# Hybrid decoder trunk: the four block sums of each up-weight pair in the second gated network made by transfers that add

## The chip, the cores and the metric

One core of a Trainium2 chip runs the whole program. The metric is device time in microseconds (us) for one execution. The kernel before takes 1214.67 us, the median of three runs (1213.35 to 1220.85). Engines are called PE (matrix), DVE (vector), ACT (scalar), POOL (GpSimd) and SP (the engine that only issues transfers here).

## The reference, cut to what matters

Two layers of width 1024 over 512 tokens: a state-space mixer, a gated network, an attention mixer, a gated network, each normed and with a residual. The change touches the gated networks, `conv_ffn`:

```python
def conv_ffn(h, w_up, conv_w, conv_b, w_down):
    up = h @ w_up                      # 1024 -> 2 * 2816
    a, b = jnp.split(up, 2, axis=-1)
    ap = jnp.pad(a, ((0, 0), (CONV_W - 1, 0), (0, 0)))
    a_conv = conv_b
    for i in range(CONV_W):
        a_conv = a_conv + ap[:, i:i + S] * conv_w[i]
    return (jax.nn.silu(a_conv) * b) @ w_down
```

Everything is float32 in and out.

## The kernel before, in words

Every float32 product is made of rounded halves: an operand is split into a high part (`w_hi`, made by ACT, a copy that rounds) and a low part (`w_lo`, made by DVE as operand minus high part), and three matmuls are added up (high by high, high by low, low by high). `put_parts` makes the two halves (L275 to L278).

The 2816 hidden features are 22 units of 128. Unit f has two tiles of up weights, 128 outputs of the convolved branch and 128 of the other, each 128 partitions by 8 blocks of 128 (512 KB). Units named in `plain` are multiplied directly (`product`, matmuls at L294, 512 columns). The other units go through `quarters` (L510): the pair of weight tiles is seen as a 2 by 2 matrix of half tiles a11, a12 (first output tile) and a21, a22 (second), the input as a 2 by 2 matrix of halves of the contraction and halves of the tokens, and seven products of half size are made instead of eight (matmuls at L550, 12 of 256 columns to a product). The scheme needs four sums of weight blocks, s1 = a21 + a22, s2 = s1 - a11, s3 = a11 - a21, s4 = a12 - s2, and four sums of input blocks t1 to t4, which `forms_x` makes once for a network (L493 to L506). The products follow each other on PE as a11, s1, a12, s2, s4, a22, s3. Tile `c` holds s1 and s2, tile `d` holds s3 and s4, both in the ring of buffers named `sums`, which has two buffers and which `forms_x` uses too. DVE makes the four sums (L518), then `parts` makes the halves of a, of c, of d and of a22. `copy` (L555) takes products out of PSUM through ACT (`nm_h`), DVE adds them (`nm_t`), and `gated` (L590) does the convolution, the gate and the split into `ghi` and `glo`.

The first network has 15 units of this kind, the second has 18, units 4 to 21 (`plain=(0, 1, 2, 3)`). The hidden units are taken in groups (6, 5, 6, 5 in the second network), and from the second group on each unit is followed by one or two column tiles of the down product of the group before (18 or 15 matmuls of 512 columns each, L294). Units 4 and 5 belong to the first group: nothing stands between them and unit 6.

Five rings set how far ahead work can run: `raw` (3 buffers, weights as loaded, L180 to L187), `w_hi` and `w_lo` (5 each), `sums`, and the PSUM ring `mm` (4 banks), of which a unit takes two (p1 and p5) and a column tile of the down product one. All engines and queues run in a fixed order, which a scheduler of the tile framework wrote at build time. SP issues all loads of the second network. POOL issues loads of modulation weights in the first network (`ada_raw`, L233) and has nothing to do in the second.

Of the kernel before, what the change touches and what calls it, by code (L numbers as in the profile page):

```python
# [8 lines left out]
F32 = mybir.dt.float32  # L9
F32R = mybir.dt.float32r  # L10
I32 = mybir.dt.int32
AF = mybir.ActivationFunctionType
ALU = mybir.AluOpType
# [4 lines left out]
P = 128  # L18
D = 1024
KT = D // P  # L20
# [46 lines left out]
def part_of(pool, shape, name, tag, bufs, aside=0):  # L67

    _, n, w = shape
    t = pool.tile([P, ROOM if bufs == WB else n * w + P], F32R, name=name, tag=tag, bufs=bufs)  # L70
    return t[:, aside:aside + n * w].rearrange("p (n w) -> p n w", w=w)


class Trunk:
# [401 lines left out]
    def forms_x(self, pool, x):  # L476

        nc = self.nc
        H, N = KT // 2, S // 2
        t1, t2 = HALVES  # L480
        normed = self.last_lo.ins
        b = []
        for j, n in enumerate(("ghi1", "glo1")):
            t = pool.tile([P, H, S], F32, name=f"x{j}", tag=n)
            for c in HALVES:
                k = slice(j * H, (j + 1) * H)
                with self.tc.issue_after(normed):
                    nc.vector.tensor_tensor(t[:, :, c], x[0][:, k, c].bitcast(F32), x[1][:, k, c].bitcast(F32), ALU.add)
                yield
            b.append(t)  # L490
        self.tx = {}

        def form(n, u, v):  # L493
            t = pool.tile([P, H, N], F32, name="sums", bufs=2)
            nc.vector.tensor_tensor(t, u, v, ALU.subtract)
            hi, lo = (pool.tile([P, H, N], F32R, name=m, bufs=4) for m in ("w_hi", "w_lo"))
            self.put_parts(hi, lo, t)
            self.tx[n] = hi, lo
            return t

        f1 = form(1, b[0][:, :, t2], b[0][:, :, t1])
        yield
        f2 = form(2, b[1][:, :, t2], f1)
        yield
        form(4, f2, b[1][:, :, t1])
        yield  # L506
        form(3, b[1][:, :, t2], b[0][:, :, t2])
        yield

    def quarters(self, pool, l, f, x, finish):  # L510

        nc = self.nc
        H, N = KT // 2, S // 2
        t1, t2 = HALVES
        a, b = (self.raw([P, KT, P], self.io["w_up"][l][2 * f + j]) for j in range(2))
        a11, a12, a21, a22 = a[:, :H], a[:, H:], b[:, :H], b[:, H:]
        c, d = (pool.tile([P, 2, H, P], F32, name="sums", bufs=2) for _ in range(2))
        sub = lambda o, u, v, op=ALU.subtract: nc.vector.tensor_tensor(o, u, v, op)  # L518
        w = {}
        copied = self.copied  # L520

        def parts(src, names, *where):
            hi, lo = (
                pool.tile([P, H * P + P], F32R, name=n, tag="e" + n)[:, ASIDE:ASIDE + H * P].rearrange("p (n w) -> p n w", w=P)
                if where else part_of(self.wpool, [P, len(names) * H, P], n, n, WB, ASIDE)
                for n in ("w_hi", "w_lo")
            )
            with self.behind(*copied):
                self.put_parts(hi, lo, src)
            for j, n in enumerate(names):  # L530
                w[n] = hi[:, j * H:(j + 1) * H], lo[:, j * H:(j + 1) * H]

        parts(a, ("a11", "a12"))
        sub(c[:, 0], a21, a22, ALU.add)
        sub(c[:, 1], c[:, 0], a11)
        parts(c.rearrange("p n k m -> p (n k) m"), ("s1", "s2"))
        sub(d[:, 1], a11, a21)
        sub(d[:, 0], a12, c[:, 1])
        parts(d.rearrange("p n k m -> p (n k) m"), ("s4", "s3"))
        parts(a22, ("a22",), pool)  # L540
        quarter = lambda k, t: tuple(v[:, k * H:(k + 1) * H, t] for v in x)
        xs = {"b11": quarter(0, t1), "b21": quarter(1, t1), "b22": quarter(1, t2)}
        for n, v in self.tx.items():
            xs[f"t{n}"] = v

        def times(o, wn, xn, first=True):
            (whi, wlo), (xhi, xlo) = w[wn], xs[xn]
            for k in range(H):
                for n, (wt, xt) in enumerate(((whi, xhi), (whi, xlo), (wlo, xhi))):
                    self.last_mm = nc.tensor.matmul(  # L550
                        o, wt[:, k], xt[:, k], start=(first and k == 0 and n == 0), stop=(k == H - 1 and n == 2),
                        skip_group_check=True,
                    )

        def copy(o, last=False):  # L555
            t = self.tmp.tile([P, N], F32, name="nm_h", bufs=4)
            a = nc.scalar.activation(t, o, AF.Copy)  # L557
            if last:
                self.copied = [a.ins]
            return t  # L560

        p1, p5 = (self.mm.tile([P, S], F32, name="mmp")[:, :N] for _ in range(2))
        p2, p4 = (self.aux.tile([P, S], F32, name="aux")[:, :N] for _ in range(2))
        oa, ob = (self.tmp.tile([P, S], F32, name="nm_t") for _ in range(2))
        times(p1, "a11", "b11")
        c1 = copy(p1)
        times(p5, "s1", "t1")
        c5 = copy(p5)
        times(p2, "a12", "b21")
        sub(oa[:, t1], p2, c1, ALU.add)  # L570
        times(p1, "s2", "t2", False)
        c2 = copy(p1, True)
        times(p5, "s4", "b22", False)
        sub(oa[:, t2], p5, c2, ALU.add)
        finish(2 * f, oa, slice(0, S))
        times(p4, "a22", "t4")
        c4 = copy(p4)
        times(p1, "s3", "t3", False)
        sub(ob[:, t2], p1, c5, ALU.add)
        sub(ob[:, t1], p1, c4)  # L580
        finish(2 * f + 1, ob, slice(0, S))

    def ffn(self, i, l, x, nxt, ticks=0, plain=None):

        nc, tc = self.nc, self.tc
        with tc.tile_pool(name=f"ffn{l}", bufs=1, reuse_waits="tile") as pool:
            self.bgpool = pool
            conv = pool.tile([P, 4, FT], F32, name="conv_wb")
            nc.sync.dma_start(conv, self.io["conv"][l])
            fill(pool, 1696)  # L590
# [5 lines left out]
            def gated(m, ps, cols):  # L596
# [25 lines left out]
            up = lambda fs, **k: self.product(  # L622
                self.io["w_up"][l], range(2 * fs[0], 2 * fs[-1] + 2), KT, x, gated,
                ticks=0 if plain else ticks, **k
            )
            last = len(groups) - 1
# [53 lines left out]
class Ew:  # L680
# [29 lines left out]
    def sub(self, a, b, out=None):  # L710
        return self.tt(a, b, ALU.subtract, out)
# [934 lines left out]
```

## Time and profile before

| what | value |
|---|---|
| median of 3 runs | 1214.67 us |
| the profiled execution, its own time | 1217.02 us |
| its span in the trace | 1215.2 us |
| granted TensorE clock, mean | 0.995 |
| PE busy | 1180.3 us, 97% |
| DVE busy | 1007.6 us, 83% |
| ACT busy | 609.8 us, 50% |
| POOL busy | 83.9 us, 7% |
| read from HBM | 175.57 MB |

The second gated network runs from about 860 us to the end of the span. In the views, "L518 DVE ... sums<-raw" is a group of instructions by its line in the program, engine, and output and input tiles; a wait "PE mmp L550 <- ACT nm_h L557" says that matmuls of line 550 stood until an instruction of line 557 on ACT was done. DMA times run from issue to landing.

### The profile page before, as it was taken

To read this page: it belongs to the slowest core of one execution; us is meant where nothing else is said; L and a number is where in the kernel's file an instruction comes from. 1 tells how busy PE (TensorE), PEld (TensorE's weight loads), DVE (VectorE), ACT (ScalarE), POOL (GpSimd) and SP (SyncE) were. 2 spreads that over 40 slices of the span, in tenths; PEclk is the share of its full clock that TensorE was granted. 3 is DMA by queue.
4 is the path that set the end of the run, shared out by engine and by line. 5 is a ranking of instruction groups with operands and counts; after the bars stand their busy time and mean duration, and the time that the engine had idled before them with its cause. 6 is when DMAs were issued, how large, how long until landed. Compare 5 with 4: busy or idle time off the path is not lost.

```text
span 1215.2 us, 20334 instructions
## 1 busy us (share of the span) xinstructions
PE 1180.3 (97%) x7793; PEld 1015.4 (84%) x7793; DVE 1007.6 (83%) x1872; ACT 609.8 (50%) x1156; POOL 83.9 (7%) x145
## 2 busy tenths in 40 slices
PE   7999999999999999999999999999999999999997
PEld 2566688898989899889899777878989999999987
DVE  7999977789899988898687578875899887888965
ACT  3644555336445454455443565654466554555543
POOL 0000000100000000000000333430000000000000
PEclk9999999999999999999999999999999999999999
DMA  9778786622455544553445543432213332333331
GB/s 348 243 250 261 233 294 220 210 77 70 136 179 164 189 155 148 169 168 106 126 153 180 172 153 130 148 108 88 89 53 113 112 119 90 103 104 109 109 100 70
DMA packets 74512, 183.81 MB, mean 151 GB/s; under 512 B 23231, under 2 KB 25631, under 8 KB 73391
## 3 DMA queue, kind: packets, MB, share of 16 engines
q1 hardware_dynamic: 68367, 161.02, 40.5%
q0 software_dynamic: 5760, 20.97, 5.4%
q8 instruction: 61, 1.00, 0.3%
q10 hardware_dynamic: 288, 0.52, 0.1%
q14 instruction: 36, 0.29, 0.1%
HBM read 175.57 MB, written 6.92 MB: 150 GB/s over the span
## 4 chain that ended last, share of the span: by engine, by line
PE 56%; issue 26%; DVE 8%; DMA 5%; ACT 2%; POOL 2%; SPq 0%; POOLq 0%; DVEq 0%; ACTq 0%
PE mmp L294 24%; PE mmp L550 11%; PE aux L550 4%; PE mmp L1366 3%; PE mmp L1174 2%; DVE w_lo L278 2%; PE mmp L1203 2%; POOL ada_raw L233 1%; PE aux L1505 1%; DMA ada_raw<-in_ada_t 1%; PE aux L1065 1%; PE mmp L1114 1%; PE aux L1057 1%; PE aux L978 1%; DMA yt<-s_yd 1%
## 5 line engine op out<-in xcount | busy, mean ns | idle before, releaser
L278 DVE TENSOR_TENSOR w_lo<-raw,w_hi 128x1024 fp32r<-128x1024 f32 (+4 forms) x173 | 183.3, 1064 | 37.6 <-ACT w_hi L277 31.8
L277 ACT ACTIVATE w_hi<-raw 128x1024 fp32r<-128x1024 f32 (+4 forms) x173 | 154.8, 904 | 105.4 <-PE mmp L294 48.6
L294 PE MATMUL mmp<-ghi,w_hi 128*128 128x512 f32 (+1 forms) x392 | 145.5, 371 | 0.0
L294 PE MATMUL mmp<-ghi,w_lo 128*128 128x512 f32 (+1 forms) x392 | 144.7, 369 | 0.7 <-DVE w_lo L278 0.6
L294 PE MATMUL mmp<-glo,w_hi 128*128 128x512 f32 (+1 forms) x392 | 145.1, 370 | 0.0
L294 PE MATMUL mmp<-a_hi,w_hi 128*128 128x512 f32 (+1 forms) x376 | 138.4, 371 | 1.5 <-ACT a_hi L433 1.5
L294 PE MATMUL mmp<-a_hi,w_lo 128*128 128x512 f32 (+1 forms) x376 | 136.2, 363 | 0.2 <-DVE w_lo L278 0.2
L294 PE MATMUL mmp<-a_lo,w_hi 128*128 128x512 f32 (+1 forms) x376 | 135.7, 362 | 0.0
L550 PE MATMUL mmp<-w_hi 128*128 128x256 f32 x396 | 109.7, 277 | 2.7 <-ACT nm_h L557 2.3
L550 PE MATMUL mmp<-w_hi,w_lo 128*128 128x256 f32 x396 | 109.5, 277 | 0.7 <-DVE w_lo L278 0.7
L550 PE MATMUL mmp<-w_lo,w_hi 128*128 128x256 f32 x396 | 109.4, 276 | 0.0
L557 ACT ACTIVATE nm_h<-mmp 128x256 f32<-128x256 f32 x99 | 37.2, 381 | 107.3 <-PE mmp L550 107.3
L278 DVE TENSOR_TENSOR w_lo<-sums,w_hi 128x1024 fp32r<-128x1024 f32 x74 | 90.0, 1219 | 0.0
L277 ACT ACTIVATE w_hi<-sums 128x1024 fp32r<-128x1024 f32 x74 | 77.0, 1055 | 23.7 <-DVE sums L518 21.7
L294 PEld LDWEIGHTS mmp<-ghi,w_lo 128*128 128x128 f32 x392 | 74.7, 190 | 13.8 <-DVE w_lo L278 1.5
L294 PEld LDWEIGHTS mmp<-ghi,w_hi 128*128 128x128 f32 x392 | 74.7, 191 | 11.5 <-ACT w_hi L277 0.2
L294 PEld LDWEIGHTS mmp<-glo,w_hi 128*128 128x128 f32 x392 | 74.8, 191 | 11.1
L294 PEld LDWEIGHTS mmp<-a_hi,w_hi 128*128 128x128 f32 x376 | 70.2, 188 | 13.8 <-issue 2.6
L294 PEld LDWEIGHTS mmp<-a_hi,w_lo 128*128 128x128 f32 x376 | 70.6, 188 | 12.2 <-DVE w_lo L278 1.2
L294 PEld LDWEIGHTS mmp<-a_lo,w_hi 128*128 128x128 f32 x376 | 70.7, 188 | 9.7
L362 DVE SCALAR_TENSOR_TENSOR h<-mmp,par,h 128x512 f32<-128x512 f32 (+1 forms) x100 | 68.0, 681 | 12.1 <-PE mmp L294 11.9
L550 PEld LDWEIGHTS mmp<-w_hi 128*128 128x128 f32 x396 | 74.3, 188 | 3.2 <-ACT nm_h L557 2.5
(319 smaller groups left out, 3077.7 us busy)
## 6 DMA issues: line engine op xcount, KB each, us to landing
raw<-in_w_up SPq DMA_DIRECT2D x88, 512.0 KB, 3.3
raw<-in_ada_w SPq DMA_DIRECT2D x40, 512.0 KB, 5.6
ada_raw<-in_ada_t POOLq DMA_DIRECT2D x40, 512.0 KB, 3.9
nf<-nfd SPq DMA_DIRECT2D x8, 1152.0 KB, 6.5
raw<-in_fox_qk SPq DMA_DIRECT2D x16, 512.0 KB, 3.7
raw<-in_w_down SPq DMA_DIRECT2D x24, 320.0 KB, 3.1
rawd<-in_w_down SPq DMA_DIRECT2D x24, 256.0 KB, 3.3
raw<-in_w_down SPq DMA_DIRECT2D x16, 384.0 KB, 3.5
```

The lines of the kernel that those rows point to most:

```text
L233: (nc.gpsimd if late else nc.sync).dma_start(ws[n], src)
L277: nc.scalar.activation(hi, src, AF.Copy)
L278: return nc.vector.tensor_tensor(lo, src, hi.bitcast(F32), ALU.subtract)
L294: self.last_mm = self.nc.tensor.matmul(o, wt, xt[:, cols], start=(k == 0 and n == 0), stop=(k == nk - 1 and n == 2),)
L362: add = self.nc.vector.scalar_tensor_tensor(self.h[:, m, cols], ps, self.par[i][:, 16 + m:17 + m], self.h[:, m, cols], op0=ALU.mult, op1=A ...
L550: self.last_mm = nc.tensor.matmul(o, wt[:, k], xt[:, k], start=(first and k == 0 and n == 0), stop=(k == H - 1 and n == 2), skip_group_che ...
L557: a = nc.scalar.activation(t, o, AF.Copy)
L978: nc.tensor.matmul(ps[:, :, cols], x[:, q, r].rearrange("p c j -> p (c j)"), both[:, :, planes, q, :], start=(r == 0), stop=(r == 1), skip ...
L1057: nc.tensor.matmul(yp[g2][:, k, :], t[:, g].rearrange("p c i -> p (c i)"), u[:, g, :], start=(k == 0), stop=False, skip_group_check=True,)
L1174: nc.tensor.matmul(ps, w[m][:, k, :], x[:, k], start=(k == 0), stop=(k == KT - 1))
L1203: nc.tensor.matmul(gps[m], wt, xt[:, k], start=(k == 0 and part == 0 and xt is yhi), stop=(k == KT - 1 and part == 1))
L1366: self.last_mm = nc.tensor.matmul(ps[q, b][:, :n], xt[:, k, tb], wt, start=(k == 0 and i == 0), stop=(k == KT - 1 and i == 2),)
```

## The change

In the second network (`l` is 1) DVE no longer makes the four sums. SP loads a11 and a21 into tile `c`, a11 and a12 into tile `d`, a22 alone into a half-filled `raw` buffer, and a as before. POOL then issues four transfers of 256 KB that add to what lies at their destination: a22 from memory onto `c[:, 1]` (giving a21 + a22), `c[:, 1]` onto `c[:, 0]` (giving a11 + a21 + a22), `c[:, 0]` onto `d[:, 1]` (giving a12 plus that), and a21 from memory onto `d[:, 0]` (giving a11 + a21). The second and third read what the one before wrote. So that all four are sums, signs are turned: t1 and the halves of t2 are negated in `forms_x`, the copies of p5 and p4 are scaled by -1, and the last two differences change sides. The first network keeps its sums on DVE, with the turned signs and in another order (`d[:, 0]` no longer waits for `c`). The ring `sums` has 2 buffers in the first network and 3 in the second.

```diff
-        def form(n, u, v):
-            t = pool.tile([P, H, N], F32, name="sums", bufs=2)
-            nc.vector.tensor_tensor(t, u, v, ALU.subtract)
+        def form(n, u, v, op=ALU.subtract, sign=1.0):
+            t = pool.tile([P, H, N], F32, name="sums", bufs=self.sums_bufs)
+            nc.vector.tensor_tensor(t, u, v, op)
...
+            if sign < 0:
+                nc.scalar.activation(hi, t, AF.Copy, scale=sign)
+                nc.vector.scalar_tensor_tensor(lo, t, sign, hi.bitcast(F32), op0=ALU.mult, op1=ALU.subtract)
+            else:
+                self.put_parts(hi, lo, t)
...
-        f1 = form(1, b[0][:, :, t2], b[0][:, :, t1])
+        f1 = form(1, b[0][:, :, t1], b[0][:, :, t2])
-        f2 = form(2, b[1][:, :, t2], f1)
+        f2 = form(2, b[1][:, :, t2], f1, ALU.add, -1.0)
...
-        a, b = (self.raw([P, KT, P], self.io["w_up"][l][2 * f + j]) for j in range(2))
-        a11, a12, a21, a22 = a[:, :H], a[:, H:], b[:, :H], b[:, H:]
-        c, d = (pool.tile([P, 2, H, P], F32, name="sums", bufs=2) for _ in range(2))
+        up = self.io["w_up"][l][2 * f:2 * f + 2]
+        a = self.raw([P, KT, P], up[0])
+        c, d = (pool.tile([P, 2, H, P], F32, name="sums", bufs=self.sums_bufs) for _ in range(2))
+        if l:
+            nc.sync.dma_start(c, up[:, :, :H].rearrange("n p k m -> p n k m"))
+            nc.sync.dma_start(d.rearrange("p n k m -> p (n k) m"), up[0])
+            a22 = self.raw([P, H, P], up[1, :, H:])
+            for o, t in ((c[:, 1], up[1, :, H:]), (c[:, 0], c[:, 1]), (d[:, 1], c[:, 0]), (d[:, 0], up[1, :, :H])):
+                nc.gpsimd.dma_start(o, t, accum_op=ALU.add)
+        else:
+            b = self.raw([P, KT, P], up[1])
+            a22 = b[:, H:]
+            sub(c[:, 1], b[:, :H], a22, ALU.add)
+            sub(c[:, 0], c[:, 1], a[:, :H], ALU.add)
...
-        sub(c[:, 0], a21, a22, ALU.add)
-        sub(c[:, 1], c[:, 0], a11)
-        parts(c.rearrange("p n k m -> p (n k) m"), ("s1", "s2"))
-        sub(d[:, 1], a11, a21)
-        sub(d[:, 0], a12, c[:, 1])
-        parts(d.rearrange("p n k m -> p (n k) m"), ("s4", "s3"))
+        parts(c.rearrange("p n k m -> p (n k) m"), ("s2", "s1"))
+        if not l:
+            sub(d[:, 0], a[:, :H], b[:, :H], ALU.add)
+            sub(d[:, 1], a[:, H:], c[:, 0], ALU.add)
+        parts(d.rearrange("p n k m -> p (n k) m"), ("s3", "s4"))
...
-        c5 = copy(p5)
+        c5 = copy(p5, sign=-1.0)
...
-        c4 = copy(p4)
+        c4 = copy(p4, sign=-1.0)
         times(p1, "s3", "t3", False)
-        sub(ob[:, t2], p1, c5, ALU.add)
-        sub(ob[:, t1], p1, c4)
+        sub(ob[:, t2], c5, p1)
+        sub(ob[:, t1], c4, p1)
...
+            self.sums_bufs = 2 + l
```

The order of instructions changes with it. Unit 6 is the first followed by a down tile, unit 7 the next; the numbers behind tile names are those of the build. What POOL issues, from unit 4 to the middle of unit 6 (`sums_9480` and `sums_9481` are c and d of unit 4, `sums_9618` and `sums_9619` of unit 5, `sums_9756` and `sums_9757` of unit 6); before, POOL has no row here:

```order
L528 DMA sums_9480<-in_w_up 128x512 [waits DMASW0_49,DVE_49,DMAHW3_49,PE_49,Activation_49]
L528 DMA sums_9480<-sums_9480 128x512 [waits DMASW1_49,DMASW0_49]
L528 DMA sums_9481<-in_w_up 128x512 [waits DMAHW4_49,DMASW2_49,DVE_49]
L528 DMA sums_9618<-in_w_up 128x512 [waits DMASW3_49,DMAHW5_49,DVE_49,Activation_49]
L528 DMA sums_9481<-sums_9480 128x512 [waits DMASW4_49,DMASW1_49]
L528 DMA sums_9618<-sums_9618 128x512 [waits DMASW5_49,DMASW3_49]
L528 DMA sums_9619<-sums_9618 128x512 [waits DMASW6_49,DMASW5_49,DMAHW1_49,DMASW4_49,DVE_49]
L528 DMA sums_9619<-in_w_up 128x512 [waits DMASW7_49]
L528 DMA sums_9756<-in_w_up 128x512 [waits DMAHW2_49,DMASW2_49,DVE_49]
L528 DMA sums_9756<-sums_9756 128x512 [waits DMASW0_49]
L528 DMA sums_9757<-sums_9756 128x512 [waits DMASW6_49,DMAHW4_49,DMASW1_49,DVE_49]
L528 DMA sums_9757<-in_w_up 128x512
```

Each row stands until the loads (DMAHW) and the earlier adds (DMASW) that it names have landed, and all later rows stand behind it.

ACT around the halves of unit 7, before (c and d are `sums_9918` and `sums_9919`; `conv_9850` and `nm_h_9867` take the results of unit 6 out):

```order
L277 ACTIVATE w_hi_9920<-raw_9914 128x1024 [waits DMAHW0_49]
L277 ACTIVATE w_hi_9936<-raw_9916 128x512 [waits DVE_49,DMAHW1_49,PE_49,Activation_49]
L600 ACTIVATE conv_9850<-nm_t_9780,conv_wb_9056 128x512 [waits DVE_49]
L557 ACTIVATE nm_h_9867<-aux_9779 128x256 [waits PE_49]
L277 ACTIVATE w_hi_9926<-sums_9918 128x1024 [waits DVE_49]
```

and in the change (c and d of unit 7 are `sums_9922` and `sums_9923`; `conv_9856` and `nm_h_9873` take the results of unit 6 out):

```order
L277 ACTIVATE w_hi_9932<-raw_9920 128x1024 [waits DMAHW7_49]
L277 ACTIVATE w_hi_9936<-sums_9922 128x1024 [waits DMAHW5_49,DMASW5_49,DMASW4_49]
L277 ACTIVATE w_hi_9940<-sums_9923 128x1024 [waits DMAHW0_49,DMASW7_49,DMASW6_49]
L615 ACTIVATE conv_9856<-nm_t_9786,conv_wb_9056 128x512 [waits DVE_49]
L571 ACTIVATE nm_h_9873<-aux_9785 128x256 [waits PE_49,Activation_49]
```

The high parts of c and d have moved ahead of the two instructions that empty unit 6, and they wait for adds on POOL's queue instead of DVE.

SP in the change, from the loads of unit 4 to those of unit 7:

```order
L524 DMA sums_9480<-in_w_up 128x2x512
L525 DMA sums_9481<-in_w_up 128x1024
L524 DMA sums_9618<-in_w_up 128x2x512
L186 DMA raw_9616<-in_w_up 128x1024
L186 DMA raw_9622<-in_w_up 128x512
L186 DMA raw_9754<-in_w_up 128x1024
L525 DMA sums_9619<-in_w_up 128x1024
L524 DMA sums_9756<-in_w_up 128x2x512
L186 DMA raw_9760<-in_w_up 128x512
L525 DMA sums_9757<-in_w_up 128x1024
L524 DMA sums_9922<-in_w_up 128x2x512
```

Before, a unit has two rows here, both `raw<-in_w_up 128x1024`; the loads into `sums` have come in between, and each waits for its buffer of three.

More of the change, by code (lines that the diff above doesn't have):

```diff
@@ L491, in forms_x @@
         self.tx = {}
-        def form(n, u, v):
-            t = pool.tile([P, H, N], F32, name="sums", bufs=2)
-            nc.vector.tensor_tensor(t, u, v, ALU.subtract)
+        def form(n, u, v, op=ALU.subtract, sign=1.0):
+            t = pool.tile([P, H, N], F32, name="sums", bufs=self.sums_bufs)
+            nc.vector.tensor_tensor(t, u, v, op)
             hi, lo = (pool.tile([P, H, N], F32R, name=m, bufs=4) for m in ("w_hi", "w_lo"))
-            self.put_parts(hi, lo, t)
+            if sign < 0:
[3 more added lines that the diff above has]
+                self.put_parts(hi, lo, t)
             self.tx[n] = hi, lo
             return t
-        f1 = form(1, b[0][:, :, t2], b[0][:, :, t1])
+        f1 = form(1, b[0][:, :, t1], b[0][:, :, t2])
         yield
-        f2 = form(2, b[1][:, :, t2], f1)
+        f2 = form(2, b[1][:, :, t2], f1, ALU.add, -1.0)
         yield
@@ L553, in times, with copy @@
                     )
-        def copy(o, last=False):
+        def copy(o, last=False, sign=1.0):
             t = self.tmp.tile([P, N], F32, name="nm_h", bufs=4)
-            a = nc.scalar.activation(t, o, AF.Copy)
+            a = nc.scalar.activation(t, o, AF.Copy, scale=sign)
             if last:
```

## Prediction

> **What bounds the kernel now.** I read the page first, for the shares of the engines and the median landing of each kind of transfer, then busy time by windows, then the waits of PE alone.
>
> ```profile
> PE 1180.3 (97%) x7793; PEld 1015.4 (84%) x7793; DVE 1007.6 (83%) x1872; ACT 609.8 (50%) x1156; POOL 83.9 (7%) x145
> ...
> raw<-in_w_up SPq DMA_DIRECT2D x88, 512.0 KB, 3.3
> ...
> ada_raw<-in_ada_t POOLq DMA_DIRECT2D x40, 512.0 KB, 3.9
> ...
> out_dram<-hg SPq DMA_DIRECT2D x4, 256.0 KB, 2.5
> ```
>
> ```profile
> 0.00:60.00 60.00, 50.75 (x213) 24.21 (x217) 51.20 (x200) 28.55 (x72) 2.66 (x22) 1.00 0.82 298
> 905.00:950.00 45.00, 45.00 (x352) 43.00 (x351) 44.04 (x66) 27.57 (x44) 0.00 (x0) 1.00 0.34 108
> 950.00:1150.00 200.00, 200.00 (x1442) 187.30 (x1441) 167.72 (x252) 104.98 (x165) 0.00 (x0) 1.00 0.34 109
> ```
>
> The columns are the window, its length, busy time of PE, weight load, DVE, ACT and POOL, granted clock, DMA share and GB/s. From 905 to 1150 us PE is busy in every microsecond at full clock, while DVE has little room at first (44.04 of 45 us) and the DMA engines much (0.34). The waits of PE from 860 us to the end, and then in the first network:
>
> ```profile
> PE mmp L294 <- ACT a_hi L433: 0.8, 1, 0.8
> PE aux L410 <- DVE rs_y L401: 0.3, 1, 0.3
> ```
>
> ```profile
> PE mmp L550 <- ACT nm_h L557: 4.3, 2, 2.3
> PE mmp L550 <- DVE w_lo L278: 2.1, 3, 0.9
> ```
>
> Neither wait of the second network (0.8 and 0.3 us) lies at a sum. So the stage that the change touches is bound by PE alone: work taken off DVE there buys nothing, and the change can only cost, by what arrives late. The chain of waits gives the timetable that the new transfers have to keep:
>
> ```profile
> 911.36 2.63 PE mmp L550 x23
> ...
> 919.43 4.08 PE mmp L550 x36
> ...
> 938.47 1.36 PE mmp L550 x12
> 939.83 4.10 PE mmp L294 x18
> 943.94 2.74 PE mmp L550 x24
> ...
> 1167.78 28.61 PE mmp L294 x156
> ```
>
> Unit 4 starts at about 911.3, unit 5 at 920.8, 1.36 us (12 matmuls) into the row of 919.43, and unit 7 at 943.94, after unit 6 and its down tile. From 911.36 to 1167.78 there are 18 units, 14.25 us each on average.
>
> **The change part by part.** Removed: 72 sums on DVE. The tile `sums` from 905 to 1168 us, with the least, the median and the longest duration in ns:
>
> ```profile
> L518 DVE TENSOR_TENSOR sums<-raw x36: 678/686/695, 907.8 to 1147.4; 128x512 f32<-128x512 f32 x36
> L277 ACT ACTIVATE w_hi<-sums x36: 1046/1063/1067, 909.7 to 1153.9; 128x1024 fp32r<-128x1024 f32 x36
> L278 DVE TENSOR_TENSOR w_lo<-sums,w_hi x36: 1208/1218/1228, 910.8 to 1155.0; 128x1024 fp32r<-128x1024 f32 x36
> L518 DVE TENSOR_TENSOR sums<-sums,raw x18: 679/683/690, 909.0 to 1148.0; 128x512 f32<-128x512 f32 x18
> L518 DVE TENSOR_TENSOR sums<-raw,sums x18: 678/684/695, 910.2 to 1153.2; 128x512 f32<-128x512 f32 x18
> ```
>
> That is 36 x 0.686 + 18 x 0.683 + 18 x 0.684 = 49 us of DVE, worth nothing here since PE waits for none of it. Also at nothing: the turned signs (an ACT copy with a scale is the same instruction; two low parts of 1.2 us become another form of DVE operation), the matmuls, which keep their order, and the first network's new order of the same number of sums. It may move the PE waits there (4.3 + 2.1) a little either way; I take 0.
>
> Added: to every unit four adds of 256 KB and 1.25 MB more of reads (c and d whole, 0.25 MB for a22 and 0.5 MB for the adds, in place of one 0.5 MB tile). In the mean unit that is 1.3 MB in 14.25 us, 92 GB/s on top of 109, and 37 more for the two adds inside SBUF: below the 298 GB/s of the first 60 us. In the opening units it is not: unit 4 to unit 5 is 9.5 us, and 2.25 MB of reads and 0.5 MB inside make 2.88 million bytes, 303 GB/s.
>
> The rows that time the rest: POOL's issue of a transfer and its landing, and the instructions that empty a unit.
>
> ```profile
> L233 POOL DMA_DIRECT2D ada_raw<-in_ada_t x40: 527/530/743, 158.4 to 555.2; - x40
> ...
> DMA to landing us min/median/max: 3.6/3.9/6.8
> ```
>
> ```profile
> L600 ACT ACTIVATE conv<-nm_t,conv_wb 128x512 f32<-128x512 f32 x18 | 14.6, 810 | 6.5 <-DVE nm_t L518 6.5
> ```
>
> ```profile
> L518 DVE TENSOR_TENSOR nm_t<-mmp,nm_h x53: 409/417/425, 919.3 to 1167.9; 128x256 f32<-128x256 f32 x53
> ...
> L557 ACT ACTIVATE nm_h<-aux x18: 359/363/385, 920.6 to 1166.5; 128x256 f32<-128x256 f32 x18
> ```
>
> Moved: the sums go from DVE to POOL's queue, where an add stands until what it needs has landed. Let A be the time from the issue of an add to its landing. The tightest place is the opening, since units 4, 5 and 6 follow each other without down tiles and the first c cannot be loaded early:
>
> ```profile
> 898.27 1.22 DVE L495 TENSOR_TENSOR sums<-sums,x 128x1024 f32<-128x1024 f32 x1
> ```
>
> This instruction is the last to read the second buffer of `sums`, which c of unit 4 takes: until 899.5. Its load lands 3.3 us later, at 902.8 (row of `raw<-in_w_up`). Then the adds c1, c0 and d1 of unit 4 (called by the half tile that they write: c1 is `c[:, 1]`) follow one another: 902.8 + 3A. The halves of that d take 1.06 on ACT and 1.22 on DVE; only then is its buffer free for c of unit 6: 3.3 us of load, then two adds (2A). POOL next issues d1 and d0 of unit 6 (2 x 0.53) and goes on with unit 7: c1, c0, then the issue of d1 (0.53) and d0 (A). d of unit 7 is there at 902.8 + 2.28 + 3.3 + 1.06 + 0.53 + 8A = 910.0 + 8A. ACT now has the high part of this d ahead of the two instructions that empty unit 6 (1.06, then 0.81 and 0.36), and DVE adds 0.42: the bank is free at 912.6 + 8A. The second product of unit 7 needs it, at 943.94 + 1.36 = 945.3, since four banks hold p1 and p5 of unit 6, one down tile and p1 of unit 7.
>
> On SP the load of c of unit 7 stands until d of unit 5 is split, and the down weights behind unit 6 stand behind it. With A = 4.5 that d is loaded from 916.3, added to from 919.6, there at 924.6 and split at 926.9; the weights land at some 930.5 and are split 2 us later. PE wants them at 939.83, so this queue has 7 us to spare.
>
> So PE comes late by **8A - 32.7 us**, once, and not at all below A = 4.1. After unit 7 the down tiles give room back: POOL's loop of a unit is two adds one behind the other and two issues, 2A + 1.06, against 14.25.
>
> No row shows an add. Lower bound: a plain 256 KB transfer, 2.5 us from SP, plus what POOL takes over SP at 512 KB (3.9 - 3.3), 3.1 us. Upper bound: the slowest POOL landing of 512 KB, 6.8 us, because an add of 256 KB reads 512 KB (source and destination). The nearest row is that same transfer at its median, 3.9 us; between the quiet and the busy stage it goes to 4.7:
>
> ```profile
> raw<-in_ada_w SPq DMA_DIRECT2D x20, 512.0 KB, 5.2
> ada_raw<-in_ada_t POOLq DMA_DIRECT2D x9, 512.0 KB, 4.7
> ```
>
> These two rows are from 60 to 275 us. I take A = 4.5, nearer the busy one, as the opening is busy: 8 x 4.5 - 32.7 = 3.3 us. With the bounds: 0 and 21.7 us. The Trainium skill, "DMA: Bandwidth & Descriptors", section "Anatomy of one DMA — SWDGE (gpsimd) path", has a fit of 2.0 us plus bytes over 436 GB/s for a transfer issued from GpSimd; by it A would be 2.6 us for 256 KB, the lateness none and the time that of the first rival. The trace is slower than that fit: it gives 3.2 us for 512 KB where the POOL row has 3.9.
>
> The sum: the profiled execution took 1217.02 us, 2.35 above the median of the runs; 1217.02 + 3.3 = 1220.3 on its footing, 1214.67 + 3.3 = **1218.0 us** on that of the median.
>
> **The rivals.** *Adds as quick as copies* (A from 3.1 to 4.1): no wait anywhere, 1214.7 us. For it: the loads of the stage are quiet now. Against it: the opening doubles to triples the traffic.
>
> *A slow opening* (the other side): adds of 5.5 us and loads of 5.2, as in the busy stage, give 8 x 5.5 - 32.7 + 2 x 1.9 = 15.1 us, 1229.8 us. It ends slower by over 1% from A = 5.1 with such loads, from 5.6 with loads of 3.3. For it: 303 GB/s asked for in the opening; against it: the rates of the busy rows lasted over hundreds of microseconds, here over 20.
>
> *POOL's loop as the bound.* If an add goes as two passes of 512 KB (2 x 3.9 = 7.8 us), a unit takes 2 x 7.8 + 1.06 = 16.7 us instead of 14.25: 18 x 2.45 = 44 us, 1259 us. It decides from A = 6.6. For it: two adds of every unit depend on one another; against it: the slowest of 40 landings is 6.8.
>
> *A better order in the first network*: all PE waits at its units go, 6.4 us, 1208.3 us. For it: one sum no longer waits for another; against it: DVE does as many.
>
> **How the numbers follow.** One per cent, about what a measurement of this kernel can tell from no change, is 12.1 us. Chances: the forecast (A between 4.1 and about 5.1, 1215 to 1226 us) 0.36, quick adds 0.27, slow opening 0.20, POOL's loop 0.12, the better order 0.05. No case reaches 1% faster; I leave 0.02 of the last for more than its price. Within 1%: 0.36 + 0.27 + 0.03 = 0.66. Slower: 0.20 + 0.12 = 0.32. The range goes from 1207, just below the better order, to 1239, a slow opening at A = 6.6 (8 x 6.6 - 32.7 + 3.8 = 23.9); POOL's loop is left out above.
>
> **What would show it.** The landing of `sums<-sums` in the DMA view is A. Right: about 4.5 us; PE waits of some 3 us in all at units 4 to 7 between 911 and 950 us and none after; DVE busy down by some 49 us; POOL issuing 72 adds of about 0.53 us. Wrong: waits of PE that go on past 960 us (the loop), a span that grows in the first network, or matmuls of another pace. The forecast falls if A is above 5.6, if an add holds POOL much longer than its issue, or if loads slow down beside the adds.

## The result, and the profile after

The changed kernel takes **1246.59 us** (median of 3 runs, 1244.96 to 1248.95), the kernel before 1214.67 us: ratio 1.0255, with a 95% interval from 1.0228 to 1.0282. It is 32 us slower; 1218.0 had been forecast. The profiled execution took 1244.96 us, its span is 1243.2 us against 1215.2, and the mean granted clock fell from 0.995 to 0.986.

The page of the change, engines and transfers (KB each, median us from issue to landing), and then the line of POOL's DMA queue (packets, MB, share of 16 engines):

```profile
PE 1192.2 (96%) x7793; PEld 1025.5 (82%) x7793; DVE 965.2 (78%) x1800; ACT 608.1 (49%) x1156; POOL 146.0 (12%) x217
...
sums<-in_w_up SPq DMA_DIRECT2D x36, 512.0 KB, 4.8
...
sums<-in_w_up POOLq DMA_DIRECT2D x36, 256.0 KB, 6.8
sums<-sums POOLq DMA_DIRECT2D x36, 256.0 KB, 4.8
```

```profile
q0 software_dynamic: 16128, 39.85, 14.1%
```

The same line of the page of the kernel before:

```profile
q0 software_dynamic: 5760, 20.97, 5.4%
```

DVE lost its 72 sums, and with them 42 us of busy time where 49 had been forecast; nothing came of it. An add of 256 KB lands in 6.8 us when it reads memory and in 4.8 us when it reads SBUF (medians). The two queue lines give what adds cost the DMA engines: 14.1% of 1243.2 less 5.4% of 1215.2 is 109.7 us of all sixteen, 1.52 us for each of 72 (the time that their packets took, in a crowded stage).

Busy time by windows (columns as in the prediction), PE's waits from 905 us on, and how long POOL is held by an issue (ns, least, median, longest):

```profile
905.00:950.00 45.00, 33.07 (x233) 31.08 (x232) 20.56 (x30) 17.38 (x29) 11.78 (x15) 0.89 0.82 204
950.00:1150.00 200.00, 193.53 (x1344) 181.09 (x1343) 129.96 (x192) 99.77 (x159) 43.57 (x51) 0.97 0.87 219
```

```profile
PE mmp L564 <- ACT nm_h L571: 13.3, 4, 5.3
PE mmp L564 <- ACT w_hi L277: 4.6, 1, 4.6
PE mmp L564 <- DVE w_lo L278: 0.5, 1, 0.5
```

```profile
L528 POOL DMA_DIRECT2D sums<-in_w_up x36: 860/1198/1550, 901.9 to 1170.4; - x36
L528 POOL DMA_DIRECT2D sums<-sums x36: 849/857/877, 908.7 to 1169.8; - x36
```

Before, PE had no idle time in these windows, at clock 1.00 and a DMA share of 0.34. Now it stands for 45 - 33.07 + 200 - 193.53 = 18.4 us, and the clock costs about 45 x 0.11 + 200 x 0.03 = 11 us more. Together 29 us, against 28.0 in the span. The busy time of PE says the same of the clock: 1192.2 us against 1180.3 for the same 7793 matmuls, 11.9 us more. The waits are few: unit 4 (4.6 and 0.5 us), then one each at units 5, 6 and 7 (1.55, 5.27 and 2.59 us), and one at unit 16 (3.87 us). Those of units 5, 6, 7 and 16 all come before the fourth product, which goes into the bank of the first. Between 975 and 1100 us PE waits for nothing.

Unit 4 to unit 7 in the change, as POOL issued it (start, length, then in brackets the idle time before the row and what ended it by the profile), and how long all 72 adds took to land:

```profile
901.91 0.91 POOL L528 DMA_DIRECT2D sums<-in_w_up  x1 [80.56 <-DMA sums<-in_w_up]
908.68 0.86 POOL L528 DMA_DIRECT2D sums<-sums  x1 [5.86 <-DMA sums<-in_w_up]
...
914.45 0.86 POOL L528 DMA_DIRECT2D sums<-sums  x1 [3.15 <-DMA sums<-sums]
...
924.50 0.87 POOL L528 DMA_DIRECT2D sums<-in_w_up  x1 [0.34 <-issue]
931.62 0.85 POOL L528 DMA_DIRECT2D sums<-sums  x1 [6.25 <-DMA sums<-in_w_up]
935.39 0.86 POOL L528 DMA_DIRECT2D sums<-sums  x1 [2.92 <-DVE w_lo L278]
...
939.18 0.86 POOL L528 DMA_DIRECT2D sums<-in_w_up  x1 [2.05 <-DVE w_lo L278]
945.60 0.85 POOL L528 DMA_DIRECT2D sums<-sums  x1 [5.56 <-DMA sums<-in_w_up]
949.45 0.86 POOL L528 DMA_DIRECT2D sums<-sums  x1 [3.00 <-DVE w_lo L278]
949.98 1.20 POOL L528 DMA_DIRECT2D sums<-in_w_up  x1
```

```profile
DMA to landing us min/median/max: 3.2/6.0/9.5
```

These rows are c1, c0 and d1 of unit 4, then c1, c0 and d1 of unit 6 and c1, c0, d1, d0 of unit 7. Where the profile names DVE (935.39, 949.45), the row reads what the add before it wrote, which had been issued 3.8 us earlier; I read these as waits for that landing. The rows of ACT that follow are the high parts of d of units 4, 6 and 7, that of c of unit 7 (951.74), and, behind that of d of unit 6, the copy that frees its first product (947.12). Below them stand SP's loads of c of units 6, 7 and 9:

```profile
917.88 1.06 ACT L277 ACTIVATE w_hi<-sums 128x1024 fp32r<-128x1024 f32 x1 [2.30 <-issue]
...
943.94 1.06 ACT L277 ACTIVATE w_hi<-sums 128x1024 fp32r<-128x1024 f32 x1 [6.72 <-issue]
...
947.12 0.37 ACT L571 ACTIVATE nm_h<-mmp 128x256 f32<-128x256 f32 x1
...
951.74 1.05 ACT L277 ACTIVATE w_hi<-sums 128x1024 fp32r<-128x1024 f32 x1
959.52 1.06 ACT L277 ACTIVATE w_hi<-sums 128x1024 fp32r<-128x1024 f32 x1 [6.73 <-issue]
```

```profile
920.22 0.38 SPq L524 DMA_DIRECT2D sums<-in_w_up  x1
...
933.86 0.38 SPq L524 DMA_DIRECT2D sums<-in_w_up  x1
...
964.60 0.38 SPq L524 DMA_DIRECT2D sums<-in_w_up  x1
```

PE goes on in unit 6 at 947.54 after 5.27 us, once the copy of 947.12 has freed p1 for the fourth product. That copy stands in ACT's order behind the high part of d, and d came late.

Two theories were put to the test. **Chain**: adds that follow one another on POOL, behind a ring of three buffers, are late where units of PE are short. **Crowding**: the adds fill the DMA engines (0.82 to 0.87 busy), and everything that is loaded comes late whatever the ring. Each run below was taken beside new runs of the kernel before (medians 1215.25 to 1216.76 us), and its ratio is to these.

### The profile page after: what moved, and what is told of

Read it like the earlier page. It is cut to its first block, busy times and chain, and to the rows that moved or that the text cites. A ratio compares the mean times of both kernels' runs of the same rounds, so it can differ in the third digit from the quotient of the medians.

```text
span 1243.2 us, 20607 instructions
## 1 busy us (share of the span) xinstructions
PE 1192.2 (96%) x7793; PEld 1025.5 (82%) x7793; DVE 965.2 (78%) x1800; ACT 608.1 (49%) x1156; POOL 146.0 (12%) x217
## 3 DMA queue, kind: packets, MB, share of 16 engines
q0 software_dynamic: 16128, 39.85, 14.1%
## 4 chain that ended last, share of the span: by engine, by line
PE 46%; issue 29%; DVE 10%; DMA 9%; ACT 3%; POOL 2%; SPq 0%; POOLq 0%; DVEq 0%; ACTq 0%
PE mmp L294 18%; PE mmp L564 6%; PE mmp L1381 3%; DVE w_lo L278 3%; PE mmp L1189 3%; PE aux L564 2%; DMA sums<-sums 2%; DMA sums<-in_w_up 2%; PE mmp L1218 2%; POOL ada_raw L233 1%; PE aux L1080 1%; PE aux L1520 1%; DVE conv L617 1%; PE mmp L205 1%; DMA ada_raw<-in_ada_t 1%
## 5 line engine op out<-in xcount | busy, mean ns | idle before, releaser
L564 PE MATMUL mmp<-w_hi 128*128 128x256 f32 x396 | 112.5, 284 | 18.3 <-ACT nm_h L571 13.3
L233 POOL DMA_DIRECT2D ada_raw<-in_ada_t x40 | 21.3, 534 | 531.1 <-DVE ada_s L247 364.4
L294 PEld LDWEIGHTS mmp<-a_hi,w_lo 128*128 128x128 f32 x376 | 70.6, 188 | 11.9 <-DVE w_lo L278 0.8
```

The costliest lines, as they stand in the source:

```text
L233: (nc.gpsimd if late else nc.sync).dma_start(ws[n], src)
L294: self.last_mm = self.nc.tensor.matmul(o, wt, xt[:, cols], start=(k == 0 and n == 0), stop=(k == nk - 1 and n == 2),)
L564: self.last_mm = nc.tensor.matmul(o, wt[:, k], xt[:, k], start=(first and k == 0 and n == 0), stop=(k == H - 1 and n == 2), skip_group_che ...
```

## The experiments: where the loss lies

**Adds from unit 8 on only.** Units 4 to 7 make their sums on DVE.

```diff
-        if l:
+        if l and f > 7:
             nc.sync.dma_start(c, up[:, :, :H].rearrange("n p k m -> p n k m"))
...
-        if not l:
+        if not (l and f > 7):
```

> Units 4 to 7 make their four sums on DVE, units 8 to 21 by adding transfers as in the change; signs, order of the products and the ring of three buffers as in the change. Chain theory (the serial adds on POOL's queue are late where PE's units are short, above all in the opening, and nothing else costs): the loss of units 4 to 7 (18.4 + 4.6 us) goes, that of unit 16 (6.9 us) may stay, so 1215 to 1223 us, and the clock stays at 1.00 from 905 to 1000 us. Crowding theory (the adds fill the DMA engines, 0.82 to 0.88 of them busy, and everything that is loaded comes late whatever the ring): the loss only moves to the first units that add, 8 to 10, and the time stays at 1235 to 1247 us.

Measured: 1232.17 us, ratio 1.0123 (1.0089 to 1.0157), 15 us over the kernel before. Neither range held it. The opening is clean, as the chain theory said, but stalls are left at units 9 and 16 (windows of PE and its waits, this kernel). The profiled execution took 1226.73 us, so what these lines show is no more than some 10 of the 15 us:

```profile
905.00:950.00 45.00, 45.00 (x355) 43.12 (x354) 42.41 (x63) 26.02 (x42) 1.77 (x2) 1.00 0.42 130
950.00:1150.00 200.00, 193.13 (x1346) 179.57 (x1346) 129.59 (x190) 99.93 (x159) 44.96 (x52) 0.98 0.89 222
```

```profile
PE mmp L564 <- ACT nm_h L571: 6.6, 3, 3.8
```

**Adds in units 4 to 7 only.**

```diff
-        if l:
+        if l and f < 8:
...
-        if not l:
+        if not (l and f < 8):
```

> The counterpart: units 4 to 7 by adding transfers (16 adds), units 8 to 21 on DVE. Chain theory: the loss of the opening stays whole, 18.4 + 4.6 us, that of unit 16 goes: 1235 to 1241 us. Crowding theory: 56 of the 72 adds and most of the traffic are gone, and with them most of the loss: 1217 to 1225 us.

Measured: 1237.53 us, 1.0160 (1.0121 to 1.0199), 21 us over. The chain theory's range holds it: sixteen adds of 72 make two thirds of the loss. Its window from 905 to 950 us reads like that of the change, and later PE is full again although it started late:

```profile
905.00:950.00 45.00, 32.96 (x229) 31.08 (x227) 19.53 (x28) 16.95 (x27) 11.23 (x13) 0.87 0.84 204
950.00:1150.00 200.00, 199.51 (x1410) 186.44 (x1411) 165.81 (x249) 103.78 (x165) 1.74 (x2) 0.99 0.35 110
```

The two parts, 15 + 21, make the whole, 32, within their intervals (each some 4 to 5 us either way).

## The experiments: the ring

**Four buffers of sums.** SBUF had no room for them as it was, so the filling tile went, and one of two buffers of `conv`.

```diff
-            self.sums_bufs = 2 + l
+            self.sums_bufs = 2 + 2 * l
...
-            fill(pool, 1696)
+            if not l:
+                fill(pool, 1696)
...
-                    t = pool.tile([P, S], F32, name="conv", bufs=2 if plain else 3)
+                    t = pool.tile([P, S], F32, name="conv", bufs=2 - l if plain else 3)
```

> The change with four buffers in the ring of sums in the second network instead of three; the room is taken from a filling tile and from the second buffer of the convolved branch. The load of c of unit 4 no longer waits for the last form of the input, and c of unit 6 waits for the halves of c of unit 4 instead of those of d. Chain theory: the chain of the opening loses about one add (5 to 7 us), one pair of halves' wait and some 3 us at its start, of 18.4 us, and the clock drops are fewer; POOL's queue stays serial: 1226 to 1238 us. Crowding theory: the traffic is the same, so 1243 to 1248 us.

Measured: 1236.73 us, 1.0164 (1.0118 to 1.0210). It lies in the chain's range, but the run has a second effect that nobody had asked for: its matmuls of 256 columns take 278 to 283 ns instead of 276 or 277 (medians of their groups after 975 us), so that a unit takes 9.84 us instead of 9.54, with the down tiles some 8 us in all. So it was repeated with another filling; the edit against the change, beside the same two of `sums_bufs` and `conv`:

```diff
-            fill(pool, 1696)
+            fill(pool, 160 if l else 1696)
```

> Four buffers again. In the first run with four, matmuls of the 256-column products took 282 ns instead of 276 and those of a unit 9.84 us instead of 9.54 (some 8 us over the network), though no wait was added: the filling tile that was left out had shifted all later tiles by 1696 bytes. Here 160 bytes of filling stay, a shift of 1536. If the pace hangs on where tiles lie within 512 bytes, units take 9.54 us again and the time is 1225 to 1232 us: the change less 10 us of the opening (unit 4 to the first down tile took 37.7 us instead of 46.9) and less the stall at unit 16. If the pace came from something else in that kernel, 1232 to 1240 us again.

Measured: 1231.19 us, 1.0129 (1.0093 to 1.0164), units of 9.54 us again, in the range that had been expected. The fourth buffer is worth 15 us. In the two profiled executions, which are 11 us apart, units 4 to 7 take 5 us less and unit 16 takes 7 us less; unit 16 no longer waits, the opening still does:

```profile
905.00:950.00 45.00, 36.61 (x272) 34.52 (x271) 25.07 (x37) 21.33 (x34) 12.10 (x14) 0.96 0.88 214
950.00:1150.00 200.00, 196.89 (x1390) 184.06 (x1389) 132.41 (x194) 100.53 (x161) 44.89 (x52) 0.98 0.89 229
```

**Both together**, run last: units 4 to 7 on DVE and four buffers (the edits above, with the filling of 160 bytes).

> Units 4 to 7 on DVE as in the first experiment, units 8 to 21 by adds, and four buffers of sums instead of three (with the filling of 160 bytes). It asks what the 15 us are that were left when the opening was made on DVE. If the serial adds behind a short ring are late there too, the fourth buffer lets them run a half unit further ahead: 1216 to 1223 us, PE waits below 3 us in the second network. If it is the crowding of the engines by the adds (some 0.86 to 0.92 busy), which delays the plain loads as well, a fourth buffer helps little: 1226 to 1233 us.

Measured: 1217.59 us, 1.0013 (0.9998 to 1.0028): 56 adds, and the loss is gone. PE's waits, the windows, and the transfers from 950 to 1150 us:

```profile
PE mmp L564 <- ACT nm_h L571: 2.6, 3, 1.5
```

```profile
905.00:950.00 45.00, 44.44 (x358) 42.92 (x356) 40.56 (x63) 26.38 (x44) 2.62 (x3) 1.00 0.47 136
950.00:1150.00 200.00, 197.97 (x1414) 184.89 (x1415) 135.03 (x198) 104.18 (x166) 45.86 (x53) 1.00 0.90 228
```

```profile
sums<-in_w_up SPq DMA_DIRECT2D x25, 512.0 KB, 5.8
sums<-sums POOLq DMA_DIRECT2D x27, 256.0 KB, 5.7
sums<-in_w_up POOLq DMA_DIRECT2D x26, 256.0 KB, 6.8
```

The transfers of the change in the same window:

```profile
sums<-in_w_up SPq DMA_DIRECT2D x25, 512.0 KB, 4.8
sums<-in_w_up POOLq DMA_DIRECT2D x26, 256.0 KB, 7.2
...
sums<-sums POOLq DMA_DIRECT2D x25, 256.0 KB, 4.9
```

The engines are as crowded as in the change (0.90 against 0.87). Loads of c and d and adds inside SBUF land later than there (5.8 us against 4.8, 5.7 against 4.9), adds from memory a little earlier (6.8 against 7.2). With a fourth buffer the transfers may start earlier, and PE hardly waits. So adds that land late need not make a loss, and crowding does not act whatever the ring: against the first experiment, which has the same adds and three buffers, the fourth buffer takes away 13 of the 15 us.

## The experiments: the add itself, and the crowding

**Copies in place of adds.**

```diff
-                nc.gpsimd.dma_start(o, t, accum_op=ALU.add)
+                nc.gpsimd.dma_start(o, t)
```

> The change with the four transfers of POOL as plain copies of the same 256 KB onto the same places, in the same order and with the same waits (the adding is left out). If the price lies in the adding itself (an add takes about twice the time of the engines that a copy takes: 109.7 us of all sixteen engines for 72 adds, 1.52 us each, against some 0.8 for 256 KB loaded plainly), a copy lands in 3 to 4.5 us, the eight serial steps of the opening shrink by 10 us or more, and the time is 1215 to 1228 us. If the price is the chain of eight steps whatever the operation (issue, landing, semaphore), copies land in 4.5 to 6 us and the time stays at 1238 to 1247 us.

Measured: 1225.16 us, 1.0086 (1.0062 to 1.0110). Two thirds of the loss go with the adding. Landings and the queue's line:

```profile
sums<-in_w_up POOLq DMA_DIRECT2D x36, 256.0 KB, 4.9
sums<-sums POOLq DMA_DIRECT2D x36, 256.0 KB, 4.3
```

```profile
q0 software_dynamic: 11520, 39.85, 9.5%
```

By the same sum as above a copy takes 9.5% of 1224.2 less 65.6, 50.7 us for 72, 0.70 us each against 1.52. It holds POOL for 0.54 us and not 0.86 to 1.2. The 10 us that stay lie in the opening alone, where PE waits 6.9 us before 956 us and not after: the chain is too long there even with copies.

**Adds that nobody waits for.** DVE makes all sums, with two buffers of `sums`, and POOL adds onto a tile of its own: in the first form as soon as it can, in the second let go by each unit's first product, in the third with copies. The lines of the second form are shown; the first has no `go` and stands ahead of the halves, the third has no `accum_op`.

```diff
-        if l:
+        if False:
...
+        if l:
+            if f == 4:
+                self.side = pool.tile([P, 2, H, P], F32, name="side", bufs=1)
+                nc.gpsimd.dma_start(self.side, up[:, :, :H].rearrange("n p k m -> p n k m"))
+            go = pool.tile([P, 2], F32, name="go", bufs=8)
+            nc.vector.tensor_copy(go, c1[:, :2])
+            nc.gpsimd.tensor_copy(self.side[:, :, 0, 0], go)
+            still = x[0][:, :H, :P].bitcast(F32)
+            for o, t in ((1, up[1, :, H:]), (0, still), (1, still), (0, up[1, :, :H])):
+                nc.gpsimd.dma_start(self.side[:, o], t, accum_op=ALU.add)
...
-            self.sums_bufs = 2 + l
+            self.sums_bufs = 2
```

> The sums of all units on DVE with the turned signs and two buffers as before; beside that POOL issues 72 adds of 256 KB, 36 from memory and 36 from a tile in SBUF, onto a tile that nobody reads (it is filled first by one load of 512 KB), so that their traffic is there and nothing waits for them. The extra plain loads of the change are not there. Chain theory: 1213 to 1218 us, as before, with loads a few tenths of a us slower and no PE wait from them. Crowding theory: loads come late and PE waits: 1228 us or more.

> As the run with 72 adds that nobody waits for, but each unit's four adds are let go by that unit's first product (DVE copies two numbers out of it, POOL writes them into the side tile ahead of the adds), so that they come at PE's pace, four in some 14 us, from 912 us on, and not all from 865 on. Chain theory: with the DMA engines some 0.75 busy loads still come in time: 1213 to 1221 us and PE waits below 3 us in the second network. Crowding theory: PE waits of 5 us or more in several units and 1224 us or more, as with the adds let go early (1234.23).

> The run with four transfers a unit that nobody waits for, let go at PE's pace, with plain copies of the same bytes in place of the adds. If the loss of that run (1229.33, PE waits of 5.6 us) came from the time that adds take on the DMA engines, copies take about half of it, loads of up weights land in 3.5 to 3.7 us instead of 4.0, and the time is 1214 to 1220 us. If it came from POOL, from DVE's extra instruction or from the places in the order, it stays at 1225 to 1233 us.

Measured: 1234.23 us let go early (1.0133, 1.0095 to 1.0171); 1229.33 us at PE's pace (1.0114, 1.0057 to 1.0171; its runs scatter from 1219.94 to 1236.0); 1215.35 us with copies (1.0008, 0.9979 to 1.0036). Both forms with adds took the time that the crowding theory had forecast, and not that of the chain theory; the third met its forecast. So crowding by adds does cost something where DVE makes its sums behind the three buffers of `raw` and two of `sums`, and copies of the same bytes, with the same extra instructions, cost nothing. The loads of up weights from 1000 to 1150 us, in the paced adds and in the copies:

```profile
raw<-in_w_up SPq DMA_DIRECT2D x20, 512.0 KB, 3.9
```

```profile
raw<-in_w_up SPq DMA_DIRECT2D x19, 512.0 KB, 3.3
```

Before, they took 3.2 us there. The profiled execution with paced adds took only 1219.94 us, with 5.6 us of PE waits in the network; the 14 us of the median are not seen row by row. These adds are also dearer than those of the change: half of them read short pieces of a wider tile, and these hold POOL for 1.34 us (median), where adds inside SBUF hold it for 0.86 in the change.

## The experiments: other ways to feed the adds

**Both adds from SBUF.** The second weight tile is loaded whole, and the adds read it there.

```diff
-            a22 = self.raw([P, H, P], up[1, :, H:])
-            for o, t in ((c[:, 1], up[1, :, H:]), (c[:, 0], c[:, 1]), (d[:, 1], c[:, 0]), (d[:, 0], up[1, :, :H])):
+            b = self.raw([P, KT, P], up[1])
+            a22 = b[:, H:]
+            for o, t in ((c[:, 1], a22), (c[:, 0], c[:, 1]), (d[:, 1], c[:, 0]), (d[:, 0], b[:, :H])):
```

> The second tile of up weights is loaded whole into the ring of loaded weights, as before the change, and the two adds of each unit that read memory read it from there instead; nothing else differs. Chain theory: four of the eight serial adds of the opening land in some 4.8 us instead of 6.8, so PE is late by 8 us less, and its clock drops less often: 1226 to 1238 us. If the landing of the adds from memory is only a matter of the crowded engines (bytes read per unit go from 2.25 to 2.0 MB, adds unchanged), their landings stay above 6 us and the time at 1240 to 1247 us.

Measured: 1299.19 us, 1.0697 (1.0668 to 1.0726), 53 us slower than the change although its adds are faster (4.7 and 3.4 us). Both theories missed it. My reading is from SP's waits, and no run tested it: the tile `b` has to stay in the ring of loaded weights until its last add has landed, and SP's queue, which issues every load in order, stands for that (55.1 us, a wait that the change does not have); behind it the loads of d stand for the adds inside SBUF (102.9 us against 22.6 in the change). SP's waits, 905 to 1240 us:

```profile
SPq L525 <- DMA sums<-sums: 102.9, 23, 9.7
...
SPq L186 <- DMA sums<-raw: 55.1, 9, 8.2
```

**Half of the adds.** DVE makes c0 and d1.

```diff
-            for o, t in ((c[:, 1], up[1, :, H:]), (c[:, 0], c[:, 1]), (d[:, 1], c[:, 0]), (d[:, 0], up[1, :, :H])):
+            for o, t in ((c[:, 1], up[1, :, H:]), (d[:, 0], up[1, :, :H])):
                 nc.gpsimd.dma_start(o, t, accum_op=ALU.add)
+            sub(c[:, 0], c[:, 1], c[:, 0], ALU.add)
...
-        if not l:
+        if l:
+            sub(d[:, 1], d[:, 1], c[:, 0], ALU.add)
+        else:
```

> The change with half of its adds: a22 onto c[:, 1] and a21 onto d[:, 0] by POOL, the two sums inside SBUF by DVE in place (36 instructions of some 0.69 us), everything else as in the change. Chain and crowding together: the opening has four serial adds fewer (4.8 us and 0.86 us of issue each, for 0.69 of DVE), so that at most 0 to 4 us of its 23 are left, and the DMA engines are some 0.65 to 0.75 busy instead of 0.86, so that the rest costs 3 to 8 us: 1218 to 1228 us. If the late load of c and the adds from memory are what sets the opening, and not the number of adds in a row, 1232 us or more.

Measured: 1245.72 us, 1.0265 (1.0226 to 1.0305), as slow as the change. The expectation of 1218 to 1228 fell, though not for the reason its rival gave: now DVE stands in its own order for the adds, and what empties PE's products stands behind it. That, too, is read from the waits of the profiled execution (1252.94 us) and not tested. DVE's, 905 to 1240 us:

```profile
DVE sums L522 <- DMA sums<-in_w_up: 79.8, 14, 7.1
```

**The signs alone.** All sums on DVE, two buffers.

```diff
-        if l:
+        if False:
             nc.sync.dma_start(c, up[:, :, :H].rearrange("n p k m -> p n k m"))
...
-        if not l:
+        if not (False):
...
-            self.sums_bufs = 2 + l
+            self.sums_bufs = 2
```

> The sums of both networks on DVE, two buffers, as before; only the turned signs and the new order of the sums remain. Both theories: no added waits in the second network; 1212 to 1218 us, 0.995 to 1.004 of the kernel before.

Measured: 1216.28 us, 1.0019 (0.9997 to 1.0042). Signs and the first network's new order cost nothing and bring nothing.

## Why the prediction was wrong, by its own steps

**Right.** PE bounded the network, and work taken off DVE bought nothing: the change can only cost, by lateness. With the loss removed (last run), DVE at 973.2 us against 1007.6 still gives 1217.59, no gain. The turned signs cost nothing. The first network hardly moved (PE waits 5.3 us at its units, 6.4 before). The tightest place was the opening, by the chain that the prediction wrote down.

**The step that failed is A, the time of an add, taken at 4.5 us.** The trace puts every piece of that chain beside its forecast (from the rows of POOL, ACT and SP above; c of unit 4 landed 0.6 us before the first row):

| piece | forecast us | trace us |
|---|---|---|
| c of unit 4 loaded, at | 902.8 | 901.3 |
| c1, c0 of unit 4 (2A) | 9.0 | 13.1 |
| d1 of unit 4 (A) | 4.5 | 3.4 |
| halves of that d, to SP's load | 2.28 | 2.3 |
| load of c of unit 6 | 3.3 | 4.3 |
| c1, c0 of unit 6 (2A) | 9.0 | 10.9 |
| POOL from d1 of unit 6 to c1 of unit 7 | 1.06 | 3.8 |
| c1, c0 of unit 7 (2A) | 9.0 | 10.3 |
| issue of d1, d0 of unit 7 | 5.03 | 10.1 |
| d of unit 7 there, at | 946.0 | 959.5 |

Eight adds and one issue took 47.8 us and not 36.5: an A of 5.9, above the 5.6 at which the prediction said that the forecast falls. One A for all adds hid this: half of the eight read memory and half SBUF, 6.8 and 4.8 us by their medians, 5.8 on average. The sign that the prediction named, the landing of `sums<-sums`, is 4.8 and looks right, as it leaves out the adds from memory.

With an A of 5.9 the prediction's formula gives 8 x 5.9 - 32.7 = 14.5 us, and PE's waits at units 4 to 7 are 14.5 us (18.4 less 3.87). That they agree so well is in part luck. The formula has one wait, at the second product of unit 7; the trace has five, two at unit 4, whose c came late, and one at the fourth product of each of units 5, 6 and 7. And the 3.8 us from d1 of unit 6 to c1 of unit 7 are not POOL's: SP loads c of unit 7 only at 933.86, and such a load lands in 4.8 us. The prediction gave that queue 7 us to spare. What lies beyond the 14.5 us, the clock (11 us) and unit 16 (3.87 us), was in no term.

The estimate of A leaned on POOL's plain transfers of 512 KB, on the thought that an add reads twice its bytes. Copies of 256 KB land in 3.8 us in an uncrowded stage (the side copies from memory, at a DMA share of 0.54) and in 4.9 in the change's places; adds take 6.8 there. The Trainium skill, "DMA: Bandwidth & Descriptors", section "Anatomy of one DMA — SWDGE (gpsimd) path", has a fit that gives 2.6 us for 256 KB and does not speak of adding transfers. The trace is far above it.

**The issue taken at 0.53 us** was 0.86 to 1.2, so an add does hold POOL longer than a plain transfer; that alone is small.

**The clock was not in the sum.** The lateness was added to the time as if PE then ran on at full speed. After most of its longer waits it did not. These are the windows after the wait of 5.27 us and after that in the first experiment (4 us slices around a wait of 2.44 us; the clock is the third number from the end):

```profile
945.00:955.00 10.00, 7.46 (x40) 7.46 (x41) 8.90 (x13) 6.30 (x11) 3.45 (x4) 0.66 0.64 149
```

```profile
1088.00:1092.00 4.00, 1.56 (x11) 1.36 (x11) 4.00 (x7) 2.44 (x5) 1.21 (x2) 0.88 0.58 117
1092.00:1096.00 4.00, 4.00 (x26) 4.00 (x26) 2.02 (x4) 0.39 (x1) 1.40 (x2) 0.69 1.01 255
```

That is 11 of the 29 us. The Trainium skill, "TensorE: Matmul & The Clock Gate", section "Part 1: The HAM clock gate", says that an idle window of about 3.4 us halves the array's clock until PE has been busy for about as long; had it been weighed, a wait of several us would have been priced at its length and some 1.7 to 3.4 us more, half of one or of two such windows, an estimate from that page. The trace agrees on the price: 4 x 0.12 + 4 x 0.31 = 1.7 us around the wait of 2.44 us, 10 x 0.34 = 3.4 us around that of 5.27. It does not agree on the length, as 2.44 us were enough here; the last section has more on that.

**"None after 960 us" was wrong**, and so was the loop of a unit, 2A + 1.06, as the measure of it. The adds c1 and c0 of unit 7 took 10.3 us, within that loop's 14.25. The loop that binds runs through the ring: with three buffers c of unit 9 takes the buffer of d of unit 7. SP loads c of unit 7 at 933.86; its adds and the wait for d0 last until 959.52; the halves of d follow; and SP's load of c of unit 9 starts at 964.60. That is 30.7 us for two units, 15.4 each. PE's mean is 14.25, and 14.9 from unit 7 on (943.94 to 1167.78 before, 15 units), as units 4 and 5 have no down tile. Loads of c keep this pace to the end: from unit 6 to unit 21 they start 15.4 us apart on average. PE gains on them where down tiles are short, as in units 14 and 15, and stands at unit 16. With four buffers c of unit 9 takes the buffer of c of unit 7, whose high part is made 7.8 us earlier than that of d (951.74 against 959.52), and in that run the loads of c start 14.6 us apart. The 15 us that the fourth buffer was worth fit this; no run splits them into steps.

**The rivals.** The slow opening had the mechanism that happened, but at an A of 5.5 and without the clock. POOL's loop had the right shape, a loop that is longer than PE's unit, in the wrong place. Quick adds and the better order fell. The range ended at 1239 because both the loop through the ring and the clock were left out of it.

**Open.** Three things stay open. One is how much of an add's 6.8 us is its own and how much the crowd's: paced adds that nobody read landed in 4.8 and 5.3 us at a DMA share of 0.82. Another is where the median with paced side adds loses what the waits of the profiled execution do not show. The third is why adds that nobody waits for cost 14 us there, while the 56 adds of the last run cost some 2.

## What to carry to other kernels

A transfer that adds is no free vector engine: here it took twice the DMA time of a copy, and 5 to 7 us from issue to landing where the DVE sum took 0.69. Count the loop through the ring, not only through the engine: load, adds in a row, split, and back to the buffer's next load, divided by the units that it spans; here one buffer more, and an opening left on DVE, took the loss away. And before moving work off an engine, see whether anything waits for it.

## What the runs showed that was not expected

A wait of PE can cost more than its length, and its length alone does not tell whether it will: after 2.44 us of waiting the granted clock was 0.69 for the next 4 us, and with side adds let go early 1.86 us were enough (0.62 over the next 4 us), while 2.1 us with paced side adds and 2.91 us with four buffers left it at 1.00 (the 4 us behind that last wait):

```profile
946.00:950.00 4.00, 4.00 (x37) 4.00 (x36) 4.00 (x7) 2.83 (x5) 1.73 (x2) 1.00 0.84 160
```

Shifting the tiles of a pool by 1696 bytes made matmuls of 256 columns take 278 to 283 ns instead of 276, and a shift by 1536 did not; with one buffer of `conv` instead of two they took 276 all the same. An add from memory held POOL for up to 1.55 us. And faster adds made the slowest kernel of all, by SP's waits because their source had to stay in a ring that was needed elsewhere.
